# The second feed-forward product by Strassen's scheme, in a phase of its own: activations and their sums through DRAM, and pairs of products in one PSUM bank

## The chip, the cores and the metric

The kernel runs on one core of a Trainium2 chip, written with a tile framework that places the waits and orders each engine's instructions itself. The metric is device microseconds of one execution; for the kernel before, the median of three runs is 1218.36 us (1217.72 to 1219.31).

## The reference, cut to what matters

One layer: a mixer of four head groups, an output projection, a residual with layer norm, then a feed-forward net with a second residual and layer norm. The change lies in the last line.

```python
def swiglu(h, w_in, w_out):
    g, u = jnp.split(h @ w_in, 2, axis=-1)
    return (jax.nn.silu(g) * u) @ w_out
...
        x = layer_norm(ALPHA * x + g1 * y, ln1_w[l], ln1_b[l])
        x = layer_norm(ALPHA * x + g2 * swiglu(x * (1.0 + sc2) + sh2, w_ffn_in[l], w_ffn_out[l]), ln2_w[l], ln2_b[l])
```

There are 1024 tokens of width 1024; the inner width D_FF is 2816, that is 22 blocks of 128 columns. All arrays are float32.

## The kernel before, in words

Every matmul operand is split into two parts that the matmul format carries exactly, a high part (a cast on ScalarE, ACT) and a low part (a subtraction on VectorE, DVE). One float32 product is three matmuls: high with high, high with low, low with high (PASSES). One matmul is 128 x 128 weights against 128 x 512 moving columns. `split2` (L853 the cast, L854 the subtraction) makes the two parts of weights that were loaded into a staging tile `raw`, of which there are two; the parts go to one of four tiles `whl`, or to a page. Pages are tiles of 8 KB per partition in three pools: pg (9), pg2 (4), pg3 (8).

The feed-forward net begins behind the first layer norm. Its first four blocks of 128 columns are computed plainly (`gate_up`, matmuls in L883). From block 4 on, two blocks at a time go through `gate_up2`: for the gate and then for the up projection, `strassen` computes the product of weights (two blocks by two halves of k) and activations (two halves of k by two halves of the tokens) in Winograd's form, with seven products of quarters for eight, 12 matmuls each (L1349). `a_sums` forms the sums of weights (L1330 to L1336), `b_sums`, once, those of the activations. DVE adds the products from PSUM (L1354). Silu runs on ACT (L1387); the product gate x up is made on DVE (L1392) and split at once into its two parts (cast L1393, subtraction L1394), which stay in pages.

The second product, with w_ffn_out, follows each pair of blocks (behind the first four blocks, each later pair, and for the last two pairs together). Its weights are loaded, multiplied by g2 on GpSimd (POOL, L860), split, and used as the moving operand of `mm2` (L1451): for each half c of the output columns and each of eight tiles t of 128 tokens, three matmuls per block. DVE adds the PSUM result to the residual XN (L1465). In the last group the residual add also gives the row sums (L1493), and each token tile goes through the layer norm (mean L1494, squares on ACT L1495, L1496 to L1498, then L1500 and L1501) and out to DRAM (L1502).

PSUM has eight banks: three named mm, two a, two b, one c. All loads and stores of this stage are issued by SyncE (SP) from one queue, in the order that the framework gives; an instruction that waits there holds back all behind it. The engines likewise run their own lists in order.

Of the kernel before, what the change touches and what calls it, by code (L numbers as in the profile page):

```python
# [27 lines left out]
class Slices:  # L28
    """Small tiles cut from one larger tile."""
# [18 lines left out]
def exp_acc(e, x, shape, cut):  # L48
    """exp(x) to float32 accuracy; returns exp, expm1 of the reduced argument and the power of two."""
# [18 lines left out]
def s5_pre(e, pool, tab):  # L68
    """Everything of the S5 discretization that has one column for each (direction, pair of groups)."""
    nc = e.nc  # L70
    v, a, pe = nc.vector, nc.scalar, nc.tensor
    S = Env()
# [27 lines left out]
    # the phase of one chunk of 8 steps  # L100
# [7 lines left out]
    # powers 0..8 of a_bar: [128, dp, l]  # L108
# [22 lines left out]
    # (a_bar - 1) / lam  # L131
# [18 lines left out]
    # b_bar [128, dp, ri, p] and the same spread block-diagonally over the two groups of a pair  # L150
    S.Bb = pool.tile([128, 2, 2, 8, 16], F32, name="s5Bb")      # d, ri, P, p
# [16 lines left out]
NP = 2      # pairs of groups in a unit  # L168


def s5_unit_tables(e, S, u, tp, wp):
# [46 lines left out]
    # kernel of the chunk by falling lag, then the Toeplitz matrices through DRAM  # L218
    BD = wp.tile([128, 4, NP, 32], F32, name="s5BD", tag="s5BD")             # (d ri), P, (gi p)
# [41 lines left out]
        # cos = 1 - 2 sin(pi f)^2, sin = 2 sin(pi f) (1 - 2 sin(pi f / 2)^2)  # L261
# [66 lines left out]
def s5_out(e, Yg, y0, yT, gw, gb, wp):  # L328
    """Yg [c, 7 - t, (g q)] -> y0 (two halves), yT [128 ch, 2, 1024] with the gated linear unit"""
# [44 lines left out]
def mlstm_gates(e, Gk, page, kp):  # L374
    """Gk [128 tok, 10, 16]: gate inputs with their bias, chunks of context then latents"""
# [56 lines left out]
    G.dec = kp.tile([128, 2, 2, 10], F32, name="mdec")       # (half k), pair, direction, step  # L432
# [36 lines left out]
    G.TW = kp.tile([128, 3, 2, 40], F32, name="mTW")         # exp of: e, inter weight, -m  # L469
# [5 lines left out]
def mlstm_states(e, G, kxc, vxc, kT, vx, C, wp):  # L475
    """states before each latent chunk; context in token layout [128, 2, 256], [128, 2, 4, 65]; latents kT, vx"""
# [45 lines left out]
def mlstm_chunk(e, G, c, qT, kT, vx, hb, wp):  # L522
    """latent chunk c of both directions -> hb [128, 4, 64]"""
# [57 lines left out]
def mlstm_norm(e, hb, sq, c0, nw, sig, yT, wp, NC=4):  # L581
    """hb [128, NC, 4, 64] of chunks c0.. -> yT[:, :, tokens] = norm * weight * sigmoid(o)"""
# [23 lines left out]
def sgu_consts(e, lnb, bsb, wsT, B):  # L606
    """the bias image [(2 groups) 64 c, 2, t] from the transposed spatial weights [s, g, t]"""
# [9 lines left out]
def ln_stats(e, srcs, wp, tag, n):  # L617
    """mean and 1/std of each source row ([128, n] each) -> [128, len, 2]"""
# [37 lines left out]
def conv_sums(e, wc, ws):  # L656
    """per channel: weights of the even taps plus those of the odd taps, [128, 2, 16]"""
# [26 lines left out]
def conv_norm(e, x, y, q, lnw, lnb, wp):  # L684
    """x [128 ch, 2, 16, 96], y [128 ch, 2, 1024] over it, tokens of quarter q -> silu(layer norm over the 256 channels)"""
# [24 lines left out]
PASSES = ((0, 0), (0, 1), (1, 0))       # (part of the weight, part of the activation): hi hi, hi lo, lo hi  # L710
# [10 lines left out]
def layout(x):  # L721
    """The inputs as the kernel reads them: transposed, cut into tiles, repeated; no arithmetic."""
# [5 lines left out]
    # S5: partitions (group in its pair, state)  # L728
# [11 lines left out]
    tile_ = lambda w: w.reshape(-1, 128, w.shape[1]).transpose(1, 0, 2)             # [128, k, columns]  # L740
# [9 lines left out]
    g["w2"] = f(x["w_ffn_out"][0].reshape(NFF, 128, 2, 512).transpose(2, 1, 0, 3))  # L750
# [11 lines left out]
def body(tc, A, out):  # L762
# [5 lines left out]
    with st:  # L768
# [18 lines left out]
        # ---- constants and small parameters  # L787
# [54 lines left out]
        # ---- weights: loaded, then split into two parts that float32r carries exactly  # L842
# [13 lines left out]
        def wsplit(raw, scale=None, pool_tag=None):  # L856
            """the parts of the weights (k, width), as two tiles of halves of k or one of the pool asked for: W(part, k)"""
# [18 lines left out]
        def projT(W, halves, rhs, cps=None, mm=None, ks=range(8), acc=None, first=True, last=True):  # L876
            """columns on partitions; rhs(part, half, k) and cps(part, k) move"""
# [10 lines left out]
        def projK(Ws, lhs, ps):  # L888
            """tokens on partitions; lhs(part, k) as lhsT"""
# [5 lines left out]
        # ---- both streams arrive transposed; modulated in place and split the same way  # L895
# [75 lines left out]
        # the columns of g1, sh2, sc2  # L971
# [11 lines left out]
        # ---- S5  # L983
# [30 lines left out]
        # ---- context keys, values, gates  # L1014
# [10 lines left out]
        # ---- convolution, inputs  # L1025
# [18 lines left out]
        # ---- mLSTM, inputs  # L1044
# [24 lines left out]
        C = mp.tile([128, 8, 2, 2, 65], F32, name="mC", tag="mC")     # (half k), latent chunk, pair, direction, v  # L1069
# [36 lines left out]
        # ---- spatial gating  # L1106
# [8 lines left out]
        # g1 over all partitions  # L1115
# [19 lines left out]
        # ---- output projection, first residual and layer norm  # L1135
# [5 lines left out]
        def stats(t):  # L1141
            """mean and 1 / std"""
# [74 lines left out]
        # h2 = xn * (ln1_w (1 + sc2)) + (ln1_b (1 + sc2) + sh2)  # L1217
# [9 lines left out]
        def residual(half, buf):  # L1227
            """alpha * (ln1_w x + ln1_b) in place of the normalized x"""
# [12 lines left out]
        # ---- FFN  # L1241
        # g2 over all partitions
# [282 lines left out]
```

## Time and profile before

| | |
|---|---|
| median of three runs | 1218.36 us |
| span of the profiled execution | 1216.7 us |
| busy: TensorE (PE) / DVE / ACT / POOL | 1170.0 / 968.2 / 419.5 / 71.3 us |
| matmuls of L1349 and of L1451 | 1512 and 1056, from 597.5 us on |
| end of the last matmul | 1207.7 us |

The page gives no time of its own for the profiled execution beside its span; the span is 1.66 us below the median, which is taken as what lies around it. In the rows of the trace, a timeline row gives start, length, engine, line, operation, tile written <- tiles read, shape and count, and in brackets the idle time before it with what ended it. A row of the table by stretches gives the stretch, its length, the busy time and number of instructions of PE, PE's weight loads, DVE, ACT and POOL, then the granted TensorE clock, the DMA share and the GB/s; for one line's instructions it has only the engines that run that line.

### The profile page before, as it was taken

The numbers are of one execution on the slowest core, as the hardware profiler recorded it, in microseconds if no ns is written. First come the engines' busy times: TensorE is split into PE (matmuls) and PEld (weight loads), VectorE is DVE, ScalarE is ACT, GpSimd is POOL, SyncE is SP. The second block draws the span as 40 slices with busy tenths as digits, with TensorE's granted clock in tenths as the row PEclk, the third lists the DMA queues.
The fourth block names the chain that finished last, engine by engine and source line by source line (L and its number), as shares of the span: only waits on it lengthen the run. The fifth ranks groups of instructions, "written<-read, shape, count | busy, mean of one in ns | idle before, by whom it ended". The sixth has DMA issues, their size and how long they took to land.

```text
span 1216.7 us, 15421 instructions
## 1 busy us (share of the span) xinstructions
PE 1170.0 (96%) x5803; PEld 922.9 (76%) x5803; DVE 968.2 (80%) x1902; ACT 419.5 (34%) x688; POOL 71.3 (6%) x52
## 2 busy tenths in 40 slices
PE   6999999999999999999999999999999999999987
PEld 1487788668897778678888787878787878788875
DVE  6588999988998899886866858586867676768786
ACT  1554444422336343752213132322222222323332
POOL 0010000000000000000300101010101010100110
PEclk9999999999999999999999999999999999999989
DMA  9442101121323464620111111121212121211222
GB/s 361 190 141 93 33 34 54 44 83 38 117 71 122 141 206 156 239 73 18 52 35 52 53 43 61 35 69 35 70 36 69 35 70 35 69 35 35 86 88 105
DMA packets 35213, 102.92 MB, mean 85 GB/s; under 512 B 3841, under 2 KB 8097, under 8 KB 34754
## 3 DMA queue, kind: packets, MB, share of 16 engines
q1 hardware_dynamic: 34722, 100.95, 25.2%
q8 instruction: 46, 0.75, 0.3%
q0 software_dynamic: 272, 0.70, 0.2%
q10 hardware_dynamic: 144, 0.29, 0.1%
q14 instruction: 29, 0.24, 0.1%
HBM read 96.17 MB, written 5.75 MB: 84 GB/s over the span
## 4 chain that ended last, share of the span: by engine, by line
PE 74%; DVE 17%; DMA 4%; ACT 2%; issue 2%; POOL 0%; DVEq 0%; SPq 0%; ACTq 0%; POOLq 0%
PE mm L1349 14%; PE mm L883 12%; PE mm L1451 8%; PE a L1451 6%; PE mm L1183 5%; PE b L1349 4%; PE b L1451 4%; PE b L883 4%; PE mm L892 3%; DVE whl L854 2%; PE c L1349 2%; DVE pg L1394 2%; PE c L1451 2%; DVE hs L1354 2%; DVE pg L1392 2%
## 5 line engine op out<-in xcount | busy, mean ns | idle before, releaser
L853 ACT CAST whl<-raw 128x512 fp32r<-128x512 f32 (+1 forms) x236 | 145.5, 622 | 380.6 <-PE mm L1451 153.2
L854 DVE TENSOR_TENSOR whl<-raw,whl 128x512 fp32r<-128x512 f32 (+1 forms) x236 | 165.4, 706 | 109.0 <-ACT whl L853 107.9
L883 PE MATMUL mm<-pg,whl 128*128 128x512 f32 x816 | 216.4, 404 | 0.7 <-ACT pg L1206 0.3
L883 PEld LDWEIGHTS mm<-pg,whl 128*128 128x128 f32 x816 | 146.5, 188 | 37.7 <-issue 6.1
L1349 PE MATMUL mm<-pg,whl 128*128 128x512 f32 x756 | 172.8, 389 | 0.0
L1349 PEld LDWEIGHTS mm<-pg,whl 128*128 128x128 f32 x756 | 141.9, 188 | 29.4
L1349 PE MATMUL b<-pg,whl 128*128 128x512 f32 x504 | 118.1, 389 | 0.0
L860 POOL TENSOR_TENSOR raw<-raw,g 128x1024 f32<-128x1024 f32 x22 | 61.7, 2805 | 852.4 <-DMA raw<-in_w_dram 737.0
L1349 PEld LDWEIGHTS b<-pg,whl 128*128 128x128 f32 x504 | 94.6, 188 | 19.6
L1451 PE MATMUL mm<-whl,pg 128*128 128x512 f32 x372 | 101.0, 400 | 0.0
L1451 PEld LDWEIGHTS mm<-whl,pg 128*128 128x128 f32 x372 | 72.3, 194 | 15.5
L1451 PE MATMUL a<-whl,pg 128*128 128x512 f32 x216 | 59.0, 404 | 12.8 <-DVE pg L1394 9.4
L892 PE MATMUL mm<-whl,pg 128*128 128x256 f32 (+1 forms) x448 | 63.1, 288 | 0.0
L1354 DVE TENSOR_TENSOR pg<-pg,mm 128x512 f32<-128x512 f32 x72 | 47.7, 683 | 19.0 <-PE mm L1349 18.6
L1451 PEld LDWEIGHTS a<-whl,pg 128*128 128x128 f32 x216 | 41.0, 192 | 26.1 <-DVE pg L1394 11.6
L1349 PE MATMUL c<-pg,whl 128*128 128x512 f32 x252 | 60.5, 389 | 0.0
L892 PEld LDWEIGHTS mm<-whl,pg 128*128 128x128 f32 x448 | 58.1, 190 | 1.5 <-issue 1.1
L1451 PE MATMUL b<-whl,pg 128*128 128x512 f32 x216 | 54.8, 389 | 0.0
L1349 PEld LDWEIGHTS c<-pg,whl 128*128 128x128 f32 x252 | 47.3, 188 | 9.8
L1183 PE MATMUL mm<-whl,pg 128*128 128x512 f32 x192 | 50.2, 398 | 0.3 <-DVE pg L1171 0.3
L1183 PE MATMUL mm<-pg 128*128 128x512 f32 x192 | 49.6, 401 | 0.1
L1451 PEld LDWEIGHTS b<-whl,pg 128*128 128x128 f32 x216 | 40.6, 188 | 8.4
(452 smaller groups left out, 1789.1 us busy)
## 6 DMA issues: line engine op xcount, KB each, us to landing
raw<-in_w_dram SPq DMA_DIRECT2D x66, 512.0 KB
pg<-in_wm_dram SPq DMA_DIRECT2D x16, 512.0 KB
raw<-in_wo_dram SPq DMA_DIRECT2D x16, 512.0 KB
raw<-in_wt_dram SPq DMA_DIRECT2D x14, 512.0 KB
mw<-in_w_mod_dram SPq DMA_DIRECT2D x24, 256.0 KB
vx<-in_w_mod_dram SPq DMA_DIRECT2D x24, 256.0 KB
pg<-in_x_dram SPq DMA_DIRECT2D x4, 1024.0 KB
pg<-in_w_mod_dram SPq DMA_DIRECT2D x8, 512.0 KB
```

The costliest lines, as they stand in the source:

```text
L853: a.copy(hi, r)
L854: v.tensor_tensor(lo, r, hi.bitcast(F32), op=SUB)
L860: gp.tensor_tensor(raw, raw, scale, op=MUL)
L883: pe.matmul(ps[h], lhsT=W(wi, k), rhs=rhs(hi, h, k), **f)
L892: pe.matmul(ps, lhsT=lhs(hi, k), rhs=Ws[k // 4](wi, k % 4), start=(k == 0 and n == 0), stop=(k == 7 and n == 2))
L1183: pe.matmul(ps, lhsT=Yr(hi, half, k)[:, t * 128:(t + 1) * 128], rhs=Ws[k // 2](wi, k % 2), start=(i + n == 0), stop=(i == 7 and n == 2))
L1349: pe.matmul(ps, lhsT=W[:, wi, k, :], rhs=B[b][hi][:, k], start=(k + n == 0), stop=(k == 3 and n == 2))
L1354: v.tensor_tensor(o, x, ps, op=ADD)
L1392: v.tensor_tensor(s_, c, s_, op=MUL)
L1394: v.tensor_tensor(lo(i, h), s_, hi(i, h).bitcast(F32), op=SUB)
L1451: pe.matmul(ps, lhsT=G[i][hi][:, t * 128:(t + 1) * 128], rhs=W[i // 2](wi, i % 2), start=(i + m == 0), stop=(i == n - 1 and m == 2))
```

## The change

**First product.** `strassen` computes the seven products in the order 11, T2, 21, T1, T3, 22, T4. Product 21 goes on accumulating into the PSUM bank of 11, and T4 into that of T3, so five adds of DVE are left of seven. Silu of the first quarter reads PSUM directly. `gate_up2` and `gate_up` leave silu(gate) x up as float32 in a page `s`; they no longer split it.

**Spill.** For each pair of blocks, `spill` forms four sums of the quarters of `s` on DVE (L1400 to L1403) and writes the four quarters and the four sums, 1 MB each, to a DRAM tile `gd` (L1404, L1405).

**Second product.** It no longer follows each pair. Once all blocks are done, seven products run over all eleven k (a k is one pair of blocks): each is 11 x 3 x 4 matmuls (L1476) into four PSUM banks, one for each of four token tiles. `operands` handles chunks of two k (24 matmuls; the sixth chunk has one k): it loads a piece of `gd` into a `whl` tile (L1462) and the weights into `raw` (L1436), and splits both into two pages each. The pages come in a fixed ring of five chunks (one from pg, four from pg3). For T2, three quarters of w_ffn_out are loaded for each chunk and combined on DVE (L1450, L1451) into pages that are kept; T1, T3 and T4 subtract with these (L1455).

**End.** g2 is multiplied into the results by DVE instead of into the weights by POOL (`gather`: L1494, L1495, L1497, then L1499 with the row sums). The layer norm (L1504 to L1511) of the first four token tiles runs beside product T4; in T4 the first three chunks run for all token tiles, the others tile by tile. The layout of w_ffn_out in DRAM is changed to match.

Core of the diff:

```diff
+        def spill(f, s):
+            k = f // 2
+            S = page([128, 4, 512])
+            v.tensor_tensor(S[:, 0], s[:, 0, 1], s[:, 1, 1], op=ADD)
...
+            ld(gd[0:4, :, k].rearrange("m p c -> p m c"), s.rearrange("p i h c -> p (i h) c"))
+            ld(gd[4:8, :, k].rearrange("m p c -> p m c"), S)
...
+            if b == "T2":
+                if k % 4 == 0:
+                    T2.append(page([128, 4, 512]))
+                r, x, y = w2load(3, k, n), w2load(1, k, n), w2load(0, k, n, "whl")
+                v.tensor_tensor(r, r, x, op=SUB)
+                v.tensor_tensor(t2(k, n), r, y, op=ADD)
+                return t2(k, n)
+            r = w2load({"T1": 3, "T3": 0, "T4": 2}[b], k, n)
+            x, y = (t2(k, n), r) if b == "T3" else (r, t2(k, n))
+            v.tensor_tensor(r, x, y, op=SUB)
+            return r
+
+        def operands(m, b, k, n):
+            get = next(ring)
+            out_ = []
+            x = sg.tile([128, n, 512], F32, name="whl", tag="whl", bufs=4)
+            ld(x, gd[m, :, k:k + n])
+            for r in (x, weights(b, k, n)):
+                hl = get([128, 2, n, 512], F32R)
+                split2(hl[:, 0], hl[:, 1], r)
+                out_.append(hl)
+            return out_
...
+        product2(6, "T2", q)
...
+        product2(2, "21", p, False)
+        for t in range(4):
+            gather(t, 0, p[t])
...
+        q = Q()
+        product2(7, "22", q)
+        for t in range(4):
+            gather(t, 1, vv[:, t], q[t])
+        for t in range(4):
+            gather(4 + t, 0, u2[:, t])
+            ln2(t)
+
+        O = [operands(3, "T4", k, n) for k, n in CH]
+        for (k, n), o in list(zip(CH, O))[:3]:
+            mms(p, o, k, n, range(4), False)
+        for t in range(4):
+            for (k, n), o in list(zip(CH, O))[3:]:
+                mms(p, o, k, n, (t,), False)
+            gather(4 + t, 0, p[t])
+            ln2(4 + t, t == 3)
```

Two places show how instructions move. The first is SP's queue. Before, from the first layer norm's weights to the end (`raw<-in_w_dram` are the weights of both products):

```order
L1230 DMA pg_5214<-in_ln_w_dram 128x1024
L1231 DMA pg_5214<-in_ln_b_dram 128x1024
L845 DMA raw<-in_w_dram 128x1024 x60
L1471 DMA pg_9345<-in_ln_w_dram 128x1024
L1472 DMA pg_9345<-in_ln_b_dram 128x1024
```

Now, on SP, around the border between the two phases: the last weights of the first product (L845), the weights (L1436) and activations (L1462) of the second, and the two stores of the last pair (L1404 the quarters, L1405 the sums); the last three rows belong to the first chunk of T2:

```order
L845 DMA raw<-in_w_dram 128x1024 x2
L1436 DMA raw<-in_w_dram 128x1024 x2
L1462 DMA whl<-gd 128x1024 x5
L1436 DMA raw<-in_w_dram 128x1024 x2
L1404 DMA gd<-pg 128x4x512
L1436 DMA raw<-in_w_dram 128x1024
L1436 DMA raw<-in_w_dram 128x512
L1462 DMA whl<-gd 128x512
L1462 DMA whl<-gd 128x1024
L1405 DMA gd<-pg 128x4x512
L1436 DMA raw<-in_w_dram 128x1024 x2
L1436 DMA whl<-in_w_dram 128x1024
```

The loads of product 11 stand ahead of the last stores, and those of T2 behind both.

The second place is the end of DVE's list. Before, it holds for each of the last token tiles the adds from two PSUM banks (a and mm) and the norm:

```order
L1493 SCALAR_TENSOR_TENSOR pg,pg_9348<-pg,a 128x512
L1496 TENSOR_SCALAR pg_9348<-pg_9348 128x1
L1500 SCALAR_TENSOR_TENSOR pg_4426<-pg_4426,pg_9348,pg_9345 128x1024
L1498 RECIPROCAL pg_9348<-pg_9348 128x1
L1501 SCALAR_TENSOR_TENSOR pg_4426<-pg_4426,pg_9348,pg_9345 128x1024
L1493 SCALAR_TENSOR_TENSOR pg,pg_9348<-pg,mm 128x512
L1494 TENSOR_SCALAR pg_9348<-pg_9348 128x1
```

Now, on DVE, what begins when product 22 ends in the banks a and b (hs are temporaries, g the columns of g2, Gk the row sums):

```order
L1494 TENSOR_TENSOR hs<-pg,a 128x512 x2
L854 TENSOR_TENSOR pg_9289<-raw,pg_9289 128x1024
L1495 TENSOR_TENSOR hs<-hs,g_4936 128x512 x2
L1499 SCALAR_TENSOR_TENSOR pg,Gk<-pg,hs 128x512 x2
L1494 TENSOR_TENSOR hs<-pg,b 128x512 x2
L1495 TENSOR_TENSOR hs<-hs,g_4936 128x512 x2
L854 TENSOR_TENSOR pg_9308<-whl,pg_9308 128x512
L1499 SCALAR_TENSOR_TENSOR pg,Gk<-pg,hs 128x512 x2
L1497 TENSOR_TENSOR hs<-pg_8354,g_4936 128x512 x2
L1499 SCALAR_TENSOR_TENSOR pg_4424,Gk<-pg_4424,hs 128x512 x2
L1497 TENSOR_TENSOR hs<-pg_8354,g_4936 128x512 x2
L1499 SCALAR_TENSOR_TENSOR pg_4426,Gk<-pg_4426,hs 128x512 x2
```

Twenty half-width operations now stand there in a row, and the norms of all eight token tiles, which before were spread over the whole last group, follow them.

More of the change, by code (lines that the diff above doesn't have):

```diff
@@ L1328, in a_sums @@
             yield parts(r0[:, lo])
-            yield parts(r0[:, hi])
             v.tensor_tensor(r1[:, lo], r1[:, lo], r1[:, hi], op=ADD)
@@ L1367, in strassen @@
[L1367 to L1384 removed]
+                a.copy(u2, X)
@@ new lines, in strassen @@
+            product("T2", Y)
+            add(u2, u2, Y)
+            product("21", X, False)
+            use(0, 0, X)
+            Z = e.ps("b")
+            product("T1", Z)
+            vv = e.tmp([128, 512], "hs")
+            add(vv, u2, Z)
+            W_ = e.ps("mm")
+            product("T3", W_)
+            o = out(1, 1, None)
+            add(o, vv, W_)
+            use(1, 1, o)
+            Q = e.ps("a")
+            product("22", Q)
+            o = out(0, 1, vv)
+            add(o, vv, Q)
@@ L1386, in gate, with gate_up2 @@
+            use(0, 1, o)
+            product("T4", W_, False)
+            o = out(1, 0, u2)
+            add(o, u2, W_)
+            use(1, 0, o)
+        def gate_up2(f, B, s):
             def gate(i, h, c):
-                a.activation(c, c, AF.Silu)
+                a.activation(s[:, i, h], c, AF.Silu)
             def up(i, h, c):
-                s_ = sl[:, i, h]
-                with tc.high_priority() if h > i else ExitStack():
-                    v.tensor_tensor(s_, c, s_, op=MUL)
-                    a.copy(hi(i, h), s_)
-                    v.tensor_tensor(lo(i, h), s_, hi(i, h).bitcast(F32), op=SUB)
@@ new lines, in body @@
+        pair = lambda: page([128, 2, 2, 512])
+        Ws = [gate_up_w(0), gate_up_w(1, pool_tag=page)]
+        s = pair()
+        for h in range(2):
+            for i in range(2):
+                gate_up(i, *Ws[i], s, (h,))
+        residual(1, page3)
+        sums = b_sums()
+        B = next(sums)
+        spill(0, s)
+        s = pair()
+        for i in range(2):
+            gate_up(i, *gate_up_w(2 + i), s, (0, 1))
+            next(sums)
+        spill(2, s)
+        next(sums)
+        for f in range(4, NFF, 2):
+            s = pair()
+            gate_up2(f, B, s)
+            spill(f, s)
@@ new lines, in body, with w2load, t2, weights @@
+        NK = NFF // 2
+        ring = itertools.cycle((page, page3, page3, page3, page3))
+        T2 = []
+        def w2load(q, k, n, tag="raw"):
+            r = sg.tile([128, n, 512], F32, name=tag, tag=tag, bufs=2 if tag == "raw" else 4)
+            ld(r, A["w2"][q, :, k:k + n])
+            return r
+        def t2(k, n):
+            return T2[k // 4][:, k % 4:k % 4 + n]
+        def weights(b, k, n):
+            if b in ("11", "21", "22"):
+                return w2load(("11", "12", "21", "22").index(b), k, n)
+            if b == "T2":
[8 more added lines that the diff above has]
+            v.tensor_tensor(r, x, y, op=SUB)
+            return r
@@ new lines, in operands, with mms @@
+        def operands(m, b, k, n):
[8 more added lines that the diff above has]
+            return out_
+        CH = [(k, min(2, NK - k)) for k in range(0, NK, 2)]
+        def mms(ps, ops, k0, n, ts, first):
+            Ag, Bg = ops
+            for k in range(n):
+                for m, (wi, hi) in enumerate(PASSES):
+                    for t in ts:
+                        pe.matmul(ps[t], lhsT=Ag[:, hi, k, t * 128:(t + 1) * 128], rhs=Bg[:, wi, k],
+                                  start=(first and k0 + k + m == 0), stop=(k0 + k == NK - 1 and m == 2), skip_group_check=True)
@@ new lines, in product2, with gather @@
+        def product2(m, b, ps, first=True):
+            for k, n in CH:
+                mms(ps, operands(m, b, k, n), k, n, range(4), first)
+        P = lambda: [e.ps(t) for t in ("mm", "mm", "mm", "c")]
+        Q = lambda: [e.ps(t) for t in ("a", "a", "b", "b")]
+        col_ = [slice(c * 512, (c + 1) * 512) for c in range(2)]
+        row = lambda t: XN[t // 2][:, t % 2]
+        stat = cp.tile([128, 8, 4], F32, name="Gk", tag="Gk")
+        def gather(t, c, x, y=None):
+            with tc.high_priority():
+                z = e.tmp([128, 512], "hs")
+                if y is not None:
+                    v.tensor_tensor(z, x, y, op=ADD)
+                    v.tensor_tensor(z, z, g2[:, col_[c]], op=MUL)
+                else:
+                    v.tensor_tensor(z, x, g2[:, col_[c]], op=MUL)
+                r = row(t)[:, col_[c]]
+                v.scalar_tensor_tensor(r, r, 1.0, z, op0=MUL, op1=ADD, accum_out=stat[:, t, c:c + 1])
@@ new lines, in body @@
+        p = P()
+        product2(5, "T3", p)
+        for t in range(4):
+            gather(4 + t, 1, vv[:, t], p[t])
+        l2, sq = page([128, 2, D]), page2([128, 2, D])
+        ld(l2[:, 0], A["ln2_w"].to_broadcast([128, D]))
+        ld(l2[:, 1], A["ln2_b"].to_broadcast([128, D]))
+        q = Q()
+        product2(7, "22", q)
+        for t in range(4):
+            gather(t, 1, vv[:, t], q[t])
+        for t in range(4):
+            gather(4 + t, 0, u2[:, t])
+            ln2(t)
+        O = [operands(3, "T4", k, n) for k, n in CH]
```

182 lines of the change are left out of this document (43 added, 139 removed).

## The prediction

> **What bounds the kernel now.** I read the page's busy shares first, then the table by stretches and by line for the stage from 597.5 us on, then the timeline at the joints.
>
> ```profile
> span 1216.7 us, 15421 instructions
> PE 1170.0 (96%) x5803; PEld 922.9 (76%) x5803; DVE 968.2 (80%) x1902; ACT 419.5 (34%) x688; POOL 71.3 (6%) x52
> ```
>
> The two lines of the stage, from a window for each line:
>
> ```profile
> 597.50:1208.00 610.50, 344.01 (x1512) 283.84 (x1512) 0.99 0.17 55
> 597.50:1208.00 610.50, 251.59 (x1056) 202.65 (x1055) 0.99 0.17 55
> ```
>
> The first is L1349, the second L1451. Now the timeline:
>
> ```profile
> 597.51 1.52 PE L1451 MATMUL a<-whl,pg 128*128 128x512 f32 x6
> 641.03 19.20 PE L1349 MATMUL mm<-pg,whl 128*128 128x512 f32 x84
> 660.07 5.60 PE L1349 MATMUL b<-pg,whl 128*128 128x512 f32 x24
> ...
> 1206.19 1.52 PE L1451 MATMUL mm<-whl,pg 128*128 128x512 f32 x6
> 1212.05 1.41 DVE L1501 SCALAR_TENSOR_TENSOR pg<-pg,pg,pg 128x512 f32<-128x512 f32 x2
> ```
>
> 84 matmuls take 660.07 - 641.03 = 19.04 us, 0.2267 us each. The stage has 2568 of them: 582.1 us at that pace. It lasts from 597.5 to 1207.7, 610.2 us, so TensorE bounds it and 28.1 us are lost. Behind the last matmul 9.0 us remain: the last residual add, its norm until 1213.5, and 3.2 us of the last store. Where the 28.1 go:
>
> ```profile
> L1451 PE MATMUL a<-whl,pg 128*128 128x512 f32 x216 | 59.0, 404 | 12.8 <-DVE pg L1394 9.4
> ...
> 679.75 0.50 PE L1451 MATMUL a<-whl,pg 128*128 128x512 f32 x1 [0.48 <-ACT pg L1393]
> 681.60 1.41 PE L1451 MATMUL a<-whl,pg 128*128 128x512 f32 x5 [1.35 <-DVE pg L1394]
> 682.85 1.52 PE L1451 MATMUL mm<-whl,pg 128*128 128x512 f32 x6
> ...
> 806.05 1.89 PE L1451 MATMUL a<-whl,pg 128*128 128x512 f32 x5 [1.35 <-DVE pg L1394]
> 807.74 2.68 PE L1451 MATMUL mm<-whl,pg 128*128 128x512 f32 x6
> ```
>
> 12.8 us are waits of the second product for the split of gate x up: 0.48 + 1.35 = 1.83 us for each of seven pairs. The rest, 15.3 us, is mostly slower matmuls. Behind the same 1.83 us, six matmuls take 1.52 us once and 2.68 us another time. The table by stretches has the same for a whole pair (columns: length, busy and count of PE, its weight loads, DVE, ACT, POOL, then clock):
>
> ```profile
> 641.00:703.25 62.25, 60.42 (x266) 49.49 (x264) 46.01 (x68) 16.92 (x28) 5.30 (x2) 1.00 0.17 51
> 765.48:829.30 63.82, 62.00 (x265) 50.61 (x264) 45.65 (x68) 16.80 (x28) 5.13 (x2) 0.97 0.17 50
> ```
>
> Clock 0.97 costs 1.57 us. The Trainium skill ("TensorE: Matmul & The Clock Gate", section "What's actually happening") has the clock fall only after an idle window of some 3.4 us; the trace disagrees where the shorter waits were followed by slow matmuls, and by that page my term for the clock below would be nothing, so 1.5 us less.
>
> **What goes.** 924 matmuls (7 products x 11 k x 12) stand for 1056: 132 x 0.2267 = 29.9 us. The seven waits and the slow clock behind them go too, since no matmul follows the gate x up split any more: -28.1. POOL's multiplies go; they lengthened DVE's work beside them:
>
> ```profile
> 793.87 2.67 POOL L860 TENSOR_TENSOR raw<-raw,g 128x1024 f32<-128x1024 f32 x1 [55.55 <-DMA raw<-in_w_dram]
> 794.91 2.18 DVE L1392 TENSOR_TENSOR pg<-hs,pg 128x512 f32<-128x512 f32 x1
> 798.21 2.88 DVE L1394 TENSOR_TENSOR pg<-pg 128x512 fp32r<-128x512 f32 x1
> ```
>
> **The first phase.** The prices that I use from here on:
>
> ```profile
> 538.54 2.29 DVE L1293 TENSOR_TENSOR pg<-pg,pg 128x2048 f32<-128x2048 f32 x1
> ...
> 769.60 0.69 DVE L854 TENSOR_TENSOR whl<-raw,whl 128x512 fp32r<-128x512 f32 x1 [2.25 <-ACT whl L853]
> 780.38 1.28 DVE L1354 TENSOR_TENSOR pg<-pg,mm 128x512 f32<-128x512 f32 x2
> 499.55 1.23 DVE L854 TENSOR_TENSOR pg<-raw,pg 128x1024 fp32r<-128x1024 f32 x1 [0.91 <-ACT pg L853]
> 1159.13 1.04 ACT L853 CAST pg<-raw 128x1024 fp32r<-128x1024 f32 x1 [2.85 <-POOL raw L860]
> ```
>
> A pair of blocks has 168 matmuls, 38.1 us. DVE has 40 half-width operations beside it (14 splits, 8 weight sums, 10 adds, 4 products, 4 sums for the spill): 40 x 0.69 = 27.6 us, 72%; ACT about 12. So TensorE runs without gaps: 1512 x 0.2267 = 342.7 us. The two stores of a pair stand in SP's queue behind the weight loads of the next Strassen set, so their wait for DVE holds nothing that is needed at once. At the start of the stage DVE's activation sums (some 2.3 us each) compete with the weight splits: 0.7 us, bounds 0 and 5.
>
> **The second phase.** Each product is 132 x 0.2267 = 29.9 us, a chunk of 24 matmuls 5.44. For a chunk of the products other than T2 a staging buffer is busy for its load, the subtraction, cast and low part. The load:
>
> ```profile
> 650.82 0.33 SPq L845 DMA_DIRECT2D raw<-in_w_dram  x1
> ...
> 654.32 0.69 DVE L1330 TENSOR_TENSOR raw<-raw 128x512 f32<-128x512 f32 x1 [0.82 <-DMA raw<-in_w_dram]
> ...
> 12.00:30.00 18.00, 12.83 (x35) 3.09 (x34) 16.88 (x84) 2.14 (x4) 0.00 (x0) 0.87 1.02 412
> ```
>
> A 512 KB load is used 3.5 us after its issue; at the 412 GB/s that the start of the kernel reaches, each further one adds 1.27. So 3.5 + 1.23 + 1.04 + 1.23 = 7.0 us, and with two buffers 3.5 to 4.2 per chunk: below 5.44, no wait. Where product 11 begins, weights of its first chunk split behind the last adds: 0.3; where 21 begins behind T2: 0.5.
>
> T2 is the hard one. It needs three quarters per chunk, in two staging buffers and a `whl` tile, and its loads stand behind the store of the last sums, which waits for DVE's fourth sum. Count from the end of the last matmul of the first phase. The last product of gate and up is made at 6.3 (four 1024-wide operations of product 11, the add and the product itself stand there: 4 x 1.23 + 2 x 0.69); the four sums and three more splits follow, 4 x 0.69 + 3 x 1.23, so the store can go at about 13 and the first load, whose buffer is split at 14.7, at 14.8; the sum of three is there at 23.3 and its cast at 24.4. The next chunk's first load waits for that buffer: 3.5 + 2 x 1.27 + 1.23, with small gaps 7.5 us per chunk. High parts are ready at 24.4, 31.9, 39.4, 46.9, 54.4 and, for the half chunk, 59. TensorE wants them at 30.2, 35.6, 41.1, 46.5, 51.9 and 57.4: it waits 0.4, then 2.1, **2.5 us** in all. With a period of 6.5 it would be nothing. If all four loads of a chunk land together (3.5 + 3 x 1.27 = 7.3, period 9.9), the fifth chunk is ready at 64.0 for 51.9, **12.1 us**. The staging row is nearest to 7.5. For waits of over 1.8 us I add 1.5 us of slow clock, as in the stretch at 0.97. The Trainium skill ("DMA: Bandwidth & Descriptors", section "Where 436 GB/s comes from") lets about 358 GB/s of HBM bind a core; the trace held 412 over 18 us, so I stay with that. By the page's figure the T2 wait would grow by an estimated 2 us.
>
> T4 then starts at 597.5 + 342.7 + 6 x 29.9 = 1119.7, plus 0.7 + 0.3 + 2.5 + 0.5 + 1.5 = 5.5: 1125.2.
>
> **The end.** The norm of one token tile before the change:
>
> ```profile
> 1183.27 0.69 DVE L1493 SCALAR_TENSOR_TENSOR pg<-pg,a 128x512 f32<-128x512 f32 x1 [1.09 <-PE a L1451]
> 1183.88 0.08 DVE L1493 DVE_READ_ACCUMULATOR pg<-pg,a 128x1 f32 x1
> ...
> 1183.95 1.27 DVE L1500 SCALAR_TENSOR_TENSOR pg<-pg,pg,pg 128x1024 f32<-128x1024 f32 x1
> 1185.14 0.15 DVE L1498 RECIPROCAL pg<-pg 128x1 f32<-128x1 f32 x1
> 1185.33 1.28 DVE L1501 SCALAR_TENSOR_TENSOR pg<-pg,pg,pg 128x1024 f32<-128x1024 f32 x1
> ```
>
> From the start of T4, DVE has 28 half-width operations of gather (20 at once, 8 on T4's results) at 0.61 back to back and 12 row sums at 0.1: 18.3; T4's last splits and subtractions 5.2; eight norms of 2 x 1.19 + 0.4: 22.2; 1 us of waits: **46.7**, then 3.2 for the last store. TensorE needs 29.9, and 2 more since the fifth chunk's weights are split behind those 20 operations. So DVE ends the kernel 14.7 us behind the last matmul, and 18 us lie behind it where 9.0 did.
>
> Sum: 1125.2 + 46.7 + 3.2 = 1175.1 of span, plus 1.7 (the median less the span of before, 1218.4 - 1216.7): **1177 us**, 41 less. By parts: -29.9 matmuls, -28.1 waits and clock, +5.5 new waits, +2 and +9 at the end.
>
> **Rivals.**
> - *No wait at T2.* Stores and loads come sooner than I count; DVE still bounds the end. 1177 - 2.5 - 1.5 = 1173; if also the eight operations on u2, which need nothing of product 22, got in before T4 (8 x 0.61 = 4.9) and the small waits went, 1167. For: slack of 6 us before the first chunk. Against: the order has them behind 22's.
> - *T2 starved.* Period 9.9, 12.1 us for 2.5, and slow clock behind five waits (5 for 1.5): 1190; with 3 more at the stage's start, 1193. For: four loads at once share 412 GB/s. Against: in the queue the activations come after the three quarters.
> - *Slower: the preparation of chunks bounds all seven products.* If SP's queue, where each load waits in order for its buffer and holds those behind it, makes the two staging buffers work in turn, a chunk costs 7.0 us or T2's 7.5. There are 7 x 5.5 = 38.5 chunks; it decides against the change from 5.44 + 41/38.5 = 6.5 us on. 7.0 gives 1177 - 2.5 + 38.5 x 1.56 = 1235, 7.5 gives 1254. Against: the two buffers are filled apart, and the ring of five chunks lies ahead of TensorE.
> - That the change does less than it says is excluded: 924 matmuls stand in the order.
>
> **How the numbers follow.** The forecast 0.60, no wait at T2 0.16, T2 starved 0.16, the slower case 0.05, others (a border that waits for all stores, 1185 or so) 0.03. A difference of 0.2%, 2.4 us, is about what a measurement of this kernel can tell from none. All but the slower case lie far below 1216: faster 0.94, same 0.01, slower 0.05. The range leaves out the slower case and the outer parts of the two beside the forecast, and takes 3 us below 1167 for durations that are a tenth shorter: 1164 to 1193.
>
> **What would show it.** Right: 924 matmuls of L1476 at 0.227; no idle of TensorE at the borders of pairs, clock 1.00 there; in T2 waits on casts or splits whose own idle ends with a load of weights, growing towards the last chunks; DVE without gaps for the last 45 us, and 18 us between the last matmul and the end. Wrong: idle before L1476 in every product (the slower rival), waits before L1349, DVE half idle at the end, or a clock that stays low in the second phase.

## The result, and the profile after

The changed kernel takes 1178.3 us (median of four runs, 1178.02 to 1181.31); the ratio to the kernel before is 0.968, 95% interval 0.966 to 0.970. The forecast was 1177 us, so the whole came out within 1.3 us. Its parts did not all do so. Two single executions among the experiments, of 1644 and 3934 us, are left out of all that follows. The page of the profiled execution, 1178.48 us long, first:

```profile
span 1176.7 us, 15244 instructions
PE 1133.6 (96%) x5671; PEld 896.3 (76%) x5671; DVE 932.8 (79%) x1837; ACT 446.9 (38%) x691; POOL 9.6 (1%) x30
```

TensorE has 132 matmuls fewer and is 36.4 us less busy; POOL's work of this stage is gone. The table by stretches cuts the stage at the joints: the first phase, the border, then the seven products in their order (11, T2, 21, T1, T3, 22, T4) and the end. Columns are as in the prediction (stretch and length; busy time and count of PE, its weight loads, DVE, ACT and POOL; clock; DMA share; GB/s).

```profile
597.50:942.96 345.46, 345.17 (x1521) 284.77 (x1519) 235.13 (x360) 109.41 (x180) 0.00 (x0) 1.00 0.34 114
942.96:945.87 2.91, 0.01 (x1) 0.01 (x1) 2.86 (x3) 2.91 (x5) 0.00 (x0) 0.86 0.72 210
945.87:978.73 32.86, 32.86 (x133) 26.92 (x133) 21.82 (x23) 11.39 (x13) 0.00 (x0) 0.91 0.87 303
978.73:1009.82 31.09, 30.30 (x133) 24.50 (x131) 19.33 (x19) 11.00 (x15) 0.00 (x0) 1.00 0.82 284
1009.82:1039.87 30.05, 30.05 (x133) 24.88 (x133) 23.33 (x23) 14.37 (x15) 0.00 (x0) 1.00 0.81 278
1039.87:1069.79 29.92, 29.92 (x133) 24.77 (x132) 21.76 (x29) 9.67 (x11) 0.00 (x0) 1.00 0.51 168
1069.79:1099.71 29.92, 29.92 (x133) 24.77 (x132) 23.25 (x24) 14.88 (x17) 0.00 (x0) 1.00 0.78 268
1099.71:1129.63 29.92, 29.92 (x133) 24.77 (x132) 26.18 (x35) 12.81 (x14) 0.00 (x0) 1.00 0.62 198
1129.63:1159.93 30.30, 30.30 (x133) 24.43 (x131) 30.08 (x61) 8.72 (x16) 0.00 (x0) 1.00 0.12 44
1159.93:1176.70 16.77, 0.01 (x1) 0.00 (x0) 13.52 (x29) 5.45 (x12) 0.00 (x0) 0.61 0.48 188
```

Read the lengths against 29.9 us, which a product needs. T1, T3 and 22 take exactly that. T4 takes 30.3 with DVE busy for all of it, and 16.8 us lie behind. The losses stand at two places. At the border there are 2.9 us of waiting, and 2.9 of slow matmuls in product 11 behind it, clock 0.91; in T2 there are 1.2 us. The waits of TensorE in the stage, from the timeline (in brackets the idle time, and what ended it):

```profile
621.43 3.29 PE L1344 MATMUL a<-pg,whl 128*128 128x512 f32 x12 [0.28 <-ACT whl L853]
...
945.87 1.65 PE L1476 MATMUL mm<-pg 128*128 128x512 f32 x3 [2.91 <-ACT pg L853]
...
1001.44 0.73 PE L1476 MATMUL a<-pg 128*128 128x512 f32 x2 [0.79 <-ACT pg L853]
```

None is left at the borders of pairs. What ACT did at the border between the phases:

```profile
941.93 1.05 ACT L853 CAST pg<-whl 128x1024 fp32r<-128x1024 f32 x1 [9.14 <-DMA whl<-gd]
942.88 1.03 ACT L853 CAST pg<-raw 128x1024 fp32r<-128x1024 f32 x1
943.83 1.04 ACT L853 CAST pg<-whl 128x1024 fp32r<-128x1024 f32 x1
944.77 1.04 ACT L853 CAST pg<-raw 128x1024 fp32r<-128x1024 f32 x1
```

TensorE starts at the end of the fourth cast, 945.8, not of the second. The order of ACT's list tells why:

```
L853 CAST pg3_7964<-whl_7960 128x1024
L853 CAST pg3_7967<-raw_7962 128x1024
L853 CAST pg_7930<-whl_7926 128x1024
L853 CAST pg_7933<-raw_7928 128x1024
```

By the numbers of the tiles the first two casts belong to the second chunk (pages of pg3) and the next two to the first chunk (a page of pg). The first chunk's activations were loaded first, but its casts stand behind a load that came only at 941.9.

### The profile page after: what moved, and what is told of

It is laid out like the page before. It is cut to its first block, busy times and chain, and to the rows that moved or that the text cites. A ratio compares the mean times of both kernels' runs of the same rounds, so it can differ in the third digit from the quotient of the medians.

```text
span 1176.7 us, 15244 instructions
## 1 busy us (share of the span) xinstructions
PE 1133.6 (96%) x5671; PEld 896.3 (76%) x5671; DVE 932.8 (79%) x1837; ACT 446.9 (38%) x691; POOL 9.6 (1%) x30
## 4 chain that ended last, share of the span: by engine, by line
PE 77%; DVE 12%; DMA 7%; ACT 2%; issue 1%; POOL 0%; SPq 0%; DVEq 0%; ACTq 0%; POOLq 0%
PE mm L1344 16%; PE mm L883 13%; PE a L1344 8%; PE mm L1476 5%; PE mm L1183 5%; PE b L1344 4%; PE b L883 4%; PE a L1476 3%; PE b L1476 3%; PE mm L892 3%; DMA raw<-in_w_dram 2%; PE c L1476 2%; PE b L564 1%; DVE whl L854 1%; DMA whl<-gd 1%
## 5 line engine op out<-in xcount | busy, mean ns | idle before, releaser
L1344 PE MATMUL a<-pg,whl 128*128 128x512 f32 x432 | 104.2, 390 | 0.3 <-ACT whl L853 0.3
L1344 PEld LDWEIGHTS a<-pg,whl 128*128 128x128 f32 x432 | 80.9, 188 | 17.8 <-ACT whl L853 0.7
L1476 PE MATMUL mm<-pg,pg 128*128 128x512 f32 x315 | 88.2, 390 | 0.0
L1476 PEld LDWEIGHTS mm<-pg,pg 128*128 128x128 f32 x315 | 59.0, 188 | 12.7 <-ACT pg L853 0.6
L854 DVE TENSOR_TENSOR pg<-raw,pg 128x1024 fp32r<-128x1024 f32 (+1 forms) x46 | 52.9, 1151 | 15.5 <-ACT pg L853 15.3
L892 PEld LDWEIGHTS mm<-whl,pg 128*128 128x128 f32 x448 | 58.1, 190 | 1.5 <-issue 1.1
L1344 PE MATMUL b<-pg,whl 128*128 128x512 f32 x216 | 51.9, 389 | 0.0
L1183 PE MATMUL mm<-whl,pg 128*128 128x512 f32 x192 | 50.2, 398 | 0.3 <-DVE pg L1171 0.3
L1476 PE MATMUL a<-pg,pg 128*128 128x512 f32 x156 | 48.0, 389 | 0.0
L1476 PE MATMUL b<-pg,pg 128*128 128x512 f32 x156 | 48.0, 389 | 0.0
L1344 PEld LDWEIGHTS b<-pg,whl 128*128 128x128 f32 x216 | 40.5, 188 | 8.4
```

Source lines behind the costliest of these rows:

```text
L854: v.tensor_tensor(lo, r, hi.bitcast(F32), op=SUB)
L892: pe.matmul(ps, lhsT=lhs(hi, k), rhs=Ws[k // 4](wi, k % 4), start=(k == 0 and n == 0), stop=(k == 7 and n == 2))
L1183: pe.matmul(ps, lhsT=Yr(hi, half, k)[:, t * 128:(t + 1) * 128], rhs=Ws[k // 2](wi, k % 2), start=(i + n == 0), stop=(i == 7 and n == 2))
L1344: pe.matmul(ps, lhsT=W[:, wi, k, :], rhs=B[b][hi][:, k], start=(first and k + n == 0), stop=(k == 3 and n == 2), skip_group_check=True)
L1476: pe.matmul(ps[t], lhsT=Ag[:, hi, k, t * 128:(t + 1) * 128], rhs=Bg[:, wi, k], start=(first and k0 + k + m == 0), stop=(k0 + k == NK - 1 a ...
```

## The experiments

The theory after the result: TensorE bounds the first phase; in the second phase two waits stand behind one another, the border's casts and T2's preparation, and mending the first alone hands its gain to the second; the end is bound by DVE. The rival: each of these is a cost by itself, and the end hangs on TensorE's last matmul. Absolute times differ a little between the sets of runs (the kernel before took 1219 to 1221 us beside them), so ratios to it are given; 0.968 is the changed kernel. This table has from each trace the loss of the second phase (from the end of the first phase to the start of T4, less 6 x 29.92 = 179.5 us) and the end (from the start of T4 to the end of the span). Each row is one execution. Product 11 alone took 30.67 to 32.95 us behind like waits (see the last section), so a difference of some 2 us between two losses proves nothing by itself.

| kernel | ratio (95%) | loss, us | end, us |
|---|---|---|---|
| changed kernel | 0.968 (0.966 to 0.970) | 7.2 | 47.1 |
| ring begins with pg3 | 0.971 (0.969 to 0.974) | 15.5 | 47.5 |
| one load for T2 | 0.963 (0.960 to 0.966) | 3.6 | 46.8 |
| ring and one load | 0.961 (0.959 to 0.963) | 2.8 | 47.4 |
| no g2 | 0.958 (0.956 to 0.961) | 5.9 | 39.7 |
| early gathers | 0.966 (0.963 to 0.968) | 10.2 | 42.2 |
| T2 direct | 0.964 (0.962 to 0.966) | 6.0 | 47.1 |
| ring and T2 direct | 0.962 (0.960 to 0.964) | 4.2 | 47.8 |
| ring, T2 direct, early gathers | 0.963 (0.961 to 0.965) | 7.9 | 43.2 |
| warm | 0.966 (0.964 to 0.968) | 10.9 | 47.1 |
| seven adds | 0.968 (0.965 to 0.970) | 9.2 | 47.1 |

**The order of the pools.**

```diff
-        ring = itertools.cycle((page, page3, page3, page3, page3))
+        ring = itertools.cycle((page3, page3, page3, page3, page))
```

> Edit: the ring of page pools of the second product begins with its four pg3 entries and ends with pg, so that the casts of the first chunk stand first on ACT; nothing else. Theory A (two waits in series: behind the border wait of 2.91 us stands the preparation of T2, whose chunks come no sooner): product 11 starts some 2.5 us sooner and runs at full clock, 5.5 us gained there, but T2 then waits 5 to 7 us instead of 0.8; the whole stays within 2 us of 1178. Theory B (the border is a cost by itself): 5.8 us less, 1172.5, and T2 waits under 2 us.

Measured 1185.6 us, ratio 0.971: by the ratios about 4 us slower than the changed kernel, with intervals that just touch. In the trace the second phase loses 8.3 us more; that execution, 1189.2 us, was one of the two longest of six. The border wait went: product 11 followed the first phase at once, with 0.56 us of waiting at its eighth matmul, for an add of the first phase (L1349). The waits of TensorE in the second phase, from the timeline:

```profile
994.56 0.74 PE L1476 MATMUL a<-pg 128*128 128x512 f32 x2 [2.12 <-ACT pg L853]
1001.98 0.73 PE L1476 MATMUL a<-pg,pg 128*128 128x512 f32 x2 [1.68 <-ACT pg L853]
1013.22 0.96 PE L1476 MATMUL mm<-pg,pg 128*128 128x512 f32 x3 [2.73 <-ACT pg L853]
...
1077.44 0.96 PE L1476 MATMUL mm<-pg 128*128 128x512 f32 x3 [2.47 <-ACT pg L853]
```

T2 and the start of 21 now wait 6.5 us, as theory A had it (5 to 7). Then come what it did not have: slow matmuls behind these waits (21 took 31.7 us at clock 0.95) and a new wait at T3. The chunk that uses the pg page is now T3's first, and its casts stand on ACT behind those of later chunks, as at the border before; the rows are shown below, with all three edits together. So this edit mends the border and carries its fault to T3. Theory B falls.

**One load for T2**, alone and with the ring.

```diff
-                r, x, y = w2load(3, k, n), w2load(1, k, n), w2load(0, k, n, "whl")
-                v.tensor_tensor(r, r, x, op=SUB)
-                v.tensor_tensor(t2(k, n), r, y, op=ADD)
+                r = w2load(3, k, n)
+                v.tensor_tensor(t2(k, n), r, r, op=ADD)
```

> Edit: a chunk of T2 loads one quarter of w_ffn_out instead of three and makes one operation of it instead of two (its weights are then not the sum that T2 needs). The border between the phases is unchanged. Both theories: the one wait in T2 of 0.79 us goes, about 1177.5; more than 2 us less would mean that the preparation of T2 costs something that the profile doesn't show as a wait of TensorE.

> Edit: both edits, the ring that begins with pg3 and the single load for a chunk of T2 (weights of T2 not the right sum). Theory A: now the gain of the border comes through, 2.9 of wait, 2.9 of slow clock and 0.8 of T2, 6.6 us less, 1171.7, against nearly nothing from the ring alone. Theory B: the same 1171.7, and the ring alone already has 5.8 of it. If the order of the casts is not what makes the border wait: about 1177.5.

Alone 1175.4 us, ratio 0.963: some 6 us less than the changed kernel, more than either theory had. The trace gives 3.6 of them to the second phase: T2 and 21 take 59.85 us together for 61.14, and product 11, behind a wait of 2.8 us, was slow for 0.75 us only. The rest lies ahead of the stage (it began at 597.6 instead of 599.2) and in the spread of the runs, so a cost that the profile doesn't show is neither shown nor ruled out. Of the 3.6 us, 2.2 are product 11, where the granted clock stayed at 1.00 this time. By the last section that hangs on how the wait fell, not on this edit, so 1.3 us, in T2 and 21, are the edit's own in this trace. With the ring 1173.8, ratio 0.961. The ring alone adds 8 us to the loss, 15.5 for 7.2; with a light T2 it takes 0.8 off, 2.8 for 3.6. So the ring's large loss comes only where T2 can't follow; that it gains anything beyond a light T2 alone is not shown, the intervals overlap. Both edits together gain 4.4 us in the second phase where 6.6 were expected: 1.1 us stay in product 11 (a wait of 0.8 for DVE) and 1.7 at T3.

**T2 direct**, alone and with the ring: the same products, right sums, but one staging buffer for a chunk.

```diff
-                r, x, y = w2load(3, k, n), w2load(1, k, n), w2load(0, k, n, "whl")
+                r = t2(k, n)
+                ld(r, A["w2"][3, :, k:k + n])
+                x, y = w2load(1, k, n), w2load(0, k, n, "whl")
                 v.tensor_tensor(r, r, x, op=SUB)
-                v.tensor_tensor(t2(k, n), r, y, op=ADD)
+                v.tensor_tensor(r, r, y, op=ADD)
```

> Edit: the first of T2's three quarters is loaded straight into the page in which the sum is kept, and the sum is made there in place, so that a chunk holds one staging buffer instead of two (all loads and operations stay). Theory A (staging buffers set T2's pace, one chunk per 7.2 us): the pace falls below 5.4 us and the T2 wait of 0.8 to 2.1 us goes; the border wait of 2.9 us and up to 2.9 us of slow clock stay: 1176 to 1178. Rival: the pace comes from the transfers themselves (2 MB per chunk with the activations): the T2 wait stays.

> Edit: the same and the ring that begins with pg3. Theory A: what the ring alone lost in T2 and at 21 (6.5 us of waits) is gone, as with the single load; T4 starts 182 to 183 us behind the last matmul of the first phase instead of 186.8, some 4 us less than the changed kernel: 1174. Rival (transfers): waits in T2 as with the ring alone, 1183.

Alone 1176.0 us, ratio 0.964; with the ring 1174.5, ratio 0.962, faster than the changed kernel (the intervals don't meet) and the lowest ratio of those that compute all of it. T2 alone with the direct load, by the table of stretches (product 11, then T2):

```profile
947.41:980.36 32.95, 32.95 (x132) 26.96 (x133) 23.32 (x24) 12.61 (x14) 0.00 (x0) 0.91 0.96 353
980.36:1010.28 29.92, 29.92 (x133) 24.78 (x132) 22.46 (x22) 15.51 (x19) 0.00 (x0) 1.00 0.86 314
```

T2 runs without any wait and all its loads are still there, so the staging buffers set its pace, not the transfers. The same two products with the ring as well:

```profile
942.61:973.74 31.13, 30.22 (x133) 24.70 (x132) 21.95 (x24) 12.28 (x14) 0.00 (x0) 1.00 0.92 331
973.74:1003.66 29.92, 29.92 (x133) 24.77 (x132) 24.23 (x23) 14.51 (x18) 0.00 (x0) 1.00 0.85 316
```

No wait in T2 either; what is left is 0.9 us in product 11 and, at T3, 1.5 and 0.7 us of waits that the moved pg page brings by the same order of casts.

**The end.** Without the multiplication by g2, and with four gathers earlier:

```diff
                     v.tensor_tensor(z, x, y, op=ADD)
-                    v.tensor_tensor(z, z, g2[:, col_[c]], op=MUL)
                 else:
-                    v.tensor_tensor(z, x, g2[:, col_[c]], op=MUL)
+                    z = x
```

> Edit: the multiplication with g2 is left out of the gathers of the second product (so the results are not scaled). From the start of T4 on this takes 12 half-width operations of 0.61 us from DVE, 7.3 us. If DVE bounds the end, as forecast: 7 us less, 1171. If TensorE bounds it: at most 1 us less. Before T4 nothing should change.

```diff
+        for t in range(4):
+            gather(4 + t, 0, u2[:, t])
         p = P()
         product2(5, "T3", p)
...
         for t in range(4):
-            gather(4 + t, 0, u2[:, t])
             ln2(t)
```

> Edit: the four gathers of u2 (eight half-width operations, which need nothing of product 22) stand behind T1 instead of behind 22. If DVE bounds the end and has room beside T3 (21.8 to 23.3 us busy of 29.9 in the products before 22): 8 x 0.61 = 4.9 us less, 1173.4, and no new wait of TensorE in T3. Rival: the end is bound by TensorE and the chain behind its last matmul: under 1 us less; or the moved operations delay splits in T3 and the gain is lost there.

Without g2 1169.9 us, ratio 0.958; the end is 39.7 us for 47.1, 7.4 less for the 7.3 of the 12 operations. The whole fell by more, some 12 us by the ratios: in the trace the stage began 3.7 us earlier and the second phase lost 1.3 less, which the edit doesn't touch. With early gathers the end is 42.2, 4.9 less, just the eight. So DVE bounds the end. But the whole with early gathers is 1178.7 us, ratio 0.966, where 1173.4 was expected, no measurable gain: the second phase lost 10.2 us for 7.2. T2 waited 2.1 us there and T3 0.7 for a split, and slower matmuls followed; T2's wait lies ahead of the moved operations, so they don't explain it; T3's lies behind them. All three edits together:

> Edit: the same and the early gathers of u2. DVE bounds the end, so the 4.9 us come on top: 1169 to 1170, if T3 has room for eight more operations of DVE; it waited 0.7 us for a split there when the gathers alone were moved, then 1171.

1173.9 us, ratio 0.963: no better than without the early gathers. The stretches of T1 and T3:

```profile
1032.09:1066.51 34.42, 30.08 (x133) 24.59 (x131) 26.10 (x40) 10.13 (x12) 0.00 (x0) 0.97 0.42 129
1066.51:1098.77 32.26, 32.26 (x133) 26.23 (x134) 20.49 (x22) 12.16 (x13) 0.00 (x0) 0.93 0.77 259
```

```profile
1061.26 1.22 DVE L1457 TENSOR_TENSOR raw<-pg,raw 128x1024 f32<-128x1024 f32 x1 [2.60 <-DMA raw<-in_w_dram]
```

T3 begins 4.3 us late and then runs slow for 2.3. Of the 4.6 us that the end gains over the kernel without early gathers, the second phase takes 3.7 back. My expectation (0.7 us of waiting) was wrong by a factor of six. The load that DVE awaits at 1061.3 is not the one of T3's first chunk. L1457 reads `pg,raw` for T3 alone; its first such subtraction, for the first chunk, stood at 1051.14, and the one at 1061.26 is its third. What ACT did then:

```profile
1062.58 1.04 ACT L853 CAST pg<-raw 128x1024 fp32r<-128x1024 f32 x1 [5.36 <-DVE raw L1457]
1063.53 1.99 ACT L853 CAST pg<-whl 128x1024 fp32r<-128x1024 f32 x2
1065.42 1.04 ACT L853 CAST pg<-raw 128x1024 fp32r<-128x1024 f32 x1
```

The same casts in ACT's list:

```
L853 CAST pg3_8858<-raw_8852 128x1024
L853 CAST pg3_8890<-whl_8885 128x1024
L853 CAST pg_8785<-whl_8780 128x1024
L853 CAST pg_8788<-raw_8782 128x1024
```

The pg pages are T3's first chunk, and TensorE starts behind the last of these casts. The first two casts belong to the third and fourth chunk. So weights that were subtracted at 1051.1 were cast at 1065.4, behind the third chunk's load: the fault of the border again, which the ring brought here. Without the early gathers the third chunk's cast came 27.6 us after T1's start, here 30.5. That the gathers bring this difference, by holding DVE, is argued, not shown.

**Matmuls in the border.**

```diff
         p, q = P(), Q()
+        for i in range(13):
+            pe.matmul(q[3], lhsT=B["T4"][0][:, 0, :128], rhs=B["T4"][0][:, 1], start=True, stop=True, skip_group_check=True)
```

> Edit of the changed kernel: 13 matmuls of 2.95 us whose result nobody reads stand on TensorE between the last matmul of the first phase and product 11, where it waited 2.9 us. If the slow clock in product 11 (32.9, 32.8, 31.7 and 30.7 us were seen for 29.9) comes from the wait: it lasts 29.9 to 30.2 now, and T2 gets less time ahead, so 1 to 2 us of the gain go into its wait: 1176 to 1178. If the slow clock doesn't hang on idle time: 30.7 to 32.9 again and 1178 to 1180.

1179.0 us, ratio 0.966. Product 11 took 30.6 us, between the two expectations; 30.7 was also seen behind a full wait, and the granted clock was 1.00 in both cases, so on the clock this run decides nothing. It decides the other question a second time: product 11 was 2.2 us shorter than in the changed kernel, so T2 began 2.0 us sooner after the first phase, and waited 4.8 us for 0.8, with 2.2 of slow matmuls behind it.

```profile
992.45 0.73 PE L1476 MATMUL a<-pg,pg 128*128 128x512 f32 x2 [1.57 <-ACT pg L853]
1001.41 0.73 PE L1476 MATMUL a<-pg 128*128 128x512 f32 x2 [3.21 <-ACT pg L853]
```

**The waits of the kernel before.**

```diff
-                G = [[g[:, x] for x in range(2)] for g in gT]
+                G = [[g[:, x] for x in range(2)] for g in (gT if f == NFF - 4 else (gT[0], gT[0]))]
```

> Edit of the kernel before: in the seven groups of one pair the second product reads the first block's activations for both blocks, so it no longer needs the quarter that is split last (the results then miss the second block); counts of all operations stay. Forecast's theory: the seven waits of 1.83 us go, 12.8 us, and with them the slow matmuls behind some of them, 3 x 1.6: 1200 to 1201 us. Rival 1: the slow clock doesn't hang on the waits: 1205. Rival 2: TensorE then waits for something else at the same place, POOL's multiplied weights say: over 1210.

1221.2 us beside 1220.8, ratio 0.999 (0.997 to 1.001), and the waits are still there: 9.0 us on L1394 and 2.9 on L1393, for 9.4 and 3.3. The edit missed them. The second product begins with the first block's later half, and that quarter is the one whose split is late. With the halves swapped as well:

```diff
-                    for h in (1, 0):
+                    for h in (1, 0) if f == 0 else (0, 1):
...
-                        ps = [e.ps(tag) for tag in (("a", "a", "mm", "mm") if h else ("b", "b", "c", "mm"))]
+                        ps = [e.ps(tag) for tag in (("a", "a", "mm", "mm") if h == (f == 0) else ("b", "b", "c", "mm"))]
```

> Edit of the kernel before, where the last one missed the wait (the wait is for the first block's second half, which it still read first): in the seven groups of one pair the second product reads the first block's activations for both blocks, and the half of the tokens that is ready first comes first (the results then miss the second block); all counts stay. Forecast's theory: the seven waits of 1.83 us go, 12.8 us, and with them most of the slow matmuls behind some of them, 3 x 1.6: 1200 to 1201 us for 1218. Rival 1: the slow clock doesn't hang on these waits: 1205. Rival 2: another wait takes the place: over 1210.

1198.3 us, ratio 0.982 (0.979 to 0.984), 22 us less. The starts of the first two pairs and of the last one after the seven groups:

```profile
644.58 7.64 PE L1349 MATMUL mm<-pg,whl 128*128 128x512 f32 x33
...
704.42 7.87 PE L1349 MATMUL mm<-pg,whl 128*128 128x512 f32 x34
...
1063.46 8.78 PE L1349 MATMUL mm<-pg,whl 128*128 128x512 f32 x38
```

A pair with its second product takes 704.42 - 644.58 = 59.84 us, 264 x 0.2267 within 0.01, seven times over: 418.9 us. In the trace of before the same seven take 440.4 (641.03 to 1081.46). The 21.5 us are 12.8 of waits and 8.7 of slower matmuls behind them. The slow clock does hang on the waits, and the matmuls behind them cost more than the 3 x 1.6 that I gave them, since every one of the seven restarts lost some 0.5 us as well: a pair with its wait took 62.25 us at clock 1.00, which is 59.84 + 1.83 + 0.58.

**Seven adds.**

```diff
-            add(u2, u2, Y)
-            product("21", X, False)
-            use(0, 0, X)
+            u1 = u2
+            u2 = e.tmp([128, 512], "hs")
+            add(u2, u1, Y)
+            X2 = e.ps("mm")
+            product("21", X2)
+            add(u1, u1, X2)
+            use(0, 0, u1)
...
-            product("T4", W_, False)
-            o = out(1, 0, u2)
-            add(o, u2, W_)
+            W2 = e.ps("mm")
+            product("T4", W2)
+            o = out(1, 0, u2)
+            add(u2, u2, W_)
+            add(o, u2, W2)
```

> Edit of the changed kernel: in the first product, 21 and T4 get PSUM banks of their own again and DVE adds seven products for five, 36 adds of 0.68 us more in the first phase; silu of the first quarter reads the sum in SBUF. DVE goes from 27.6 to 30.3 us per pair of 38.1 us of TensorE, so by the forecast nothing changes: within 1 us of 1178, and the first phase stays at 343.6 us. Rival: the adds stand in the chain to the last quarter, so the border between the phases grows by 0.7 to 1.4 us; or PSUM banks come free later and TensorE waits in each Strassen set, 18 x 0.7 = 12 us more.

1181.2 us, ratio 0.968 (0.965 to 0.970), the changed kernel's own. The first phase took 344.9 us with one wait of 0.65 us near its start, no wait per set, and the border wait was 3.0. The second phase of this trace lost 9.2 us for 7.2, with 3.4 us of waits in T2 and 21 for 0.8. So the pairs of products in one PSUM bank, taken alone, are worth nothing that can be measured; DVE had the room.

## Why the prediction was right, point by point

- **What goes.** Right. The products that run freely take 29.92 us for 132 matmuls, and the first phase took 343.8 us, from 599.2 to 943.0, for 342.7. The 28.1 us of waits and slow clock went as a whole; the experiment with the swapped halves takes 21.5 of them, those of the seven pairs, out of the kernel before by itself. Only the split was off. Of the 15.3 us that the prediction called mostly slower matmuls, 3.3 are waits too, in the last group, for the parts of weights; they and the slow matmuls behind them cost 6.4 us:

```profile
1160.23 0.73 PE L1451 MATMUL mm<-pg,pg 128*128 128x512 f32 x2 [1.09 <-ACT pg L853]
1163.17 2.08 PE L1451 MATMUL mm<-pg,pg 128*128 128x512 f32 x4 [2.20 <-DVE pg L854]
```

- **The first phase.** Right: no wait at any border of pairs, 0.28 us at its start. It began 1.7 us later than in the profile before, which no term had; in the eleven kernels of the table it began between 595.5 and 599.5, and what runs ahead of it is the same in all.
- **Product 11.** Wrong in size, and this is the step that failed: "weights of its first chunk split behind the last adds: 0.3". It cost 2.9 of waiting and 2.9 of slow clock. I had followed SP's and DVE's lists across the border, not ACT's, where the second chunk's casts stand ahead of the first's, and where the second chunk's load waits for a weight tile that the first phase still reads.
- **T2.** The mechanism was right: the wait stood at the fifth chunk, behind a cast that followed DVE's sum of three, which had awaited a load of weights:

```profile
997.73 1.23 DVE L1450 TENSOR_TENSOR raw<-raw 128x1024 f32<-128x1024 f32 x1 [2.67 <-DMA raw<-in_w_dram]
1000.34 1.05 ACT L853 CAST pg<-pg 128x1024 fp32r<-128x1024 f32 x1
```

  The measured 0.8 us for 2.5 is not proof of the size: TensorE came to T2 35.8 us after the first phase instead of 30.2, so the late border paid for it. With the border mended the same preparation made TensorE wait 6.5 us (ring) or 4.8 us (warm), so my 2.5 was too low for the case that I had worked out. The last sums went out 14.4 us behind the first phase's end and the first load of T2 16.4, for 13 and 14.8; after that the loads of a chunk followed one another by 9.6, 7.1 and 7.2 us, for 7.5:

```profile
957.32 0.37 SPq L1405 DMA_DIRECT2D gd<-pg  x1
959.33 2.01 SPq L1436 DMA_DIRECT2D raw<-in_w_dram  x2
...
968.90 1.59 SPq L1436 DMA_DIRECT2D raw<-in_w_dram  x2
...
976.02 1.72 SPq L1436 DMA_DIRECT2D raw<-in_w_dram  x2
...
983.23 2.97 SPq L1436 DMA_DIRECT2D raw<-in_w_dram  x2
```

- **The end.** Right: 47.1 us from the start of T4 for 49.9 forecast, T4's matmuls 30.3 of it for 31.9, 16.8 us behind them for 18, DVE busy for 30.1 of 30.3 and then 13.5 of 16.8, and two experiments move it by just the operations that they move.
- **The sum.** T4 began at 1129.6 for 1125.2: 1.7 from a later start, 0.4 in the first phase's length less its term, 2.4 more in the second phase (7.2 for 4.8). The end gave 2.8 back. The span was 1176.7 for 1175.1, so the agreement within 1.3 us is partly luck, two errors against one another.
- **The slower rival**, preparation that bounds all seven products, did not come: 21, T1, T3 and 22 run at 29.9 to 30.1 us. T2's starvation, the other rival, came where the border was mended.

## What to carry to other kernels

Where work goes from one phase to another, follow the first chunk through every engine's list, casts on ACT included: the engine that nobody suspects may hold the second chunk's work ahead of the first's. After mending such an order, look where it went: here the new ring brought the same order to T3. Before mending a wait, ask what comes next on the same chain; here mending the border alone gained nothing, and of the kernels that mend it or T2 and still compute all of it, only those with both came out faster, outside the changed kernel's interval. A wait of TensorE cost more than its length here, some 0.5 us more behind 1.83 and up to 3.0 more behind 3.0, so count the restart too.

## What the runs showed of the hardware

The price of a restart was not expected in this size or spread. Behind nearly the same wait at the border, 2.6 to 3.0 us, product 11 took 30.67, 31.66, 31.75, 32.80, 32.86 and 32.95 us in six kernels, for 29.92: 0.75 to 3.0 us more, with granted clocks from 1.00 to 0.91. Before the change, waits of 1.83 us were followed by slow groups in three of seven. The table by stretches of the kernel before shows where (columns as above):

```profile
741.94:745.36 3.42, 2.05 (x8) 1.47 (x9) 3.41 (x6) 1.64 (x3) 0.00 (x0) 1.00 0.39 144
...
803.39:806.80 3.41, 1.59 (x6) 0.84 (x5) 3.40 (x7) 1.83 (x4) 0.00 (x0) 1.00 0.56 154
806.80:810.21 3.41, 3.41 (x9) 2.65 (x9) 2.21 (x4) 1.07 (x2) 0.00 (x0) 0.50 0.38 101
...
933.09:936.50 3.41, 3.41 (x9) 2.68 (x9) 1.97 (x4) 0.83 (x2) 0.00 (x0) 0.50 0.43 114
...
1059.38:1062.79 3.41, 3.41 (x9) 2.66 (x9) 1.74 (x3) 0.62 (x1) 0.00 (x0) 0.50 0.46 153
```

The clock fell to 0.50 for 3.41 us, three times, 126.29 us apart, which is 37 times 3.413. In this stage it rose and fell only on such a grid of 3.41 us, in every trace kept. Whether the clock falls behind a wait goes, in all cases but one, with the place of the wait on this grid. Before each of the three falls, 1.70 to 1.82 of the 1.83 us lay in one step of it (3.41 less 1.59 of PE busy in the row at 803.39); in the four places without a fall, at most 1.37 (the row at 741.94). At the border it was 2.0 to 2.8 us in one step before the five falls; in the kernel with one load for T2 the wait of 2.80 us was cut into 1.49 and 1.39, and the clock stayed at 1.00. The one that doesn't fit is T2's wait with early gathers, 1.94 us in one step without a fall. The Trainium skill ("TensorE: Matmul & The Clock Gate", section "What's actually happening") has the clock fall after an idle window of about 3.4 us; here the step has that length, but up to the last matmul no step was idle for more than 2.8 us before a fall, and some 1.7 were enough.
